# A hybrid decoder layer on one core: split x kept in DRAM between two sweeps, gates written as tanh, another order in the passage to the output projection

## The chip, the cores and the metric

The kernel runs on one core of a Trainium2 chip. The metric is the device time of one execution in microseconds (us). The profile comes from one execution recorded by the hardware profiler.

## What is computed

One step of a decoder layer, on 2048 prompt tokens and 8 × 4 decode tokens with 1024 channels. Cut from the reference:

```python
xn = rms_norm(x, p['g_mix_norm'])
proj = xn @ p['w_in']                      # u_pool 256 | x_rnn 512 | g_rnn 512 | q 256
o_pool, new_pool = pool_mixer(ctx_pool, u_pool, start, p['w_pool'], p['pool_scale'])
xc, new_conv = causal_dwconv(ctx_conv, x_rnn, p['rnn_conv_w'], p['rnn_conv_b'])
h, h_last = rg_lru(xc, h0, p['w_rg_a'], p['b_rg_a'], p['w_rg_x'], p['b_rg_x'], p['rg_lambda'])
o_rnn = jax.nn.gelu(g_rnn, approximate=True) * h
o_xa = cross_attn(q, mk, mv)               # 4 heads, 256 memory tokens
mix = jnp.concatenate([group_rms(o_pool), group_rms(o_rnn), group_rms(o_xa)], axis=-1)
x = x + (mix * p['g_mix_out']) @ p['w_out']
xn = rms_norm(x, p['g_ffn_norm'])
gate_c, new_ffn = causal_dwconv(ctx_ffn, xn @ p['w_ff_gate'], p['ffn_conv_w'], p['ffn_conv_b'])
x = x + (jax.nn.gelu(gate_c, approximate=True) * (xn @ p['w_ff_up'])) @ p['w_ff_down']
# rg_lru:  r = sigmoid(xb @ w_a + b_a);  i = sigmoid(xb @ w_x + b_x)
#          log_a = -8 * r * softplus(-lam);  a = exp(log_a);  mult = sqrt(-expm1(2 * log_a))
#          h_t = a_t * h_(t-1) + mult * i * xc
```

## The kernel before

Channels lie on the 128 partitions and tokens on the free axis. The tokens are cut into 6 stages of 344 or 348 columns (`NCOL`; the 32 decode tokens lie at the start of stage 0), and two stages make a block. Every matrix product is made in fp32r from a rounded part and a rest: ACT writes the part (`hi`, tiles `ah..`, `h_w..`), DVE the rest (`lo`, tiles `al..`, `l_w..`), and PE does three matmuls, hi·hi, lo·hi and hi·lo.

The program runs through these phases; the times are read off the trace of PE:

- *First sweep*, 5 to 252 us, stages 0 to 5. `g_prep` loads x of a stage and splits it, with the gain g_mix, into 8 pairs `ahr`, `alr`. PE makes the recurrent input (`pr`, weights wr0 to wr3) and the gate branch (`pq`, wr4 to wr7). DVE and ACT do the convolution (`xc`), PE the small gate matmuls (`pg`, L452), ACT the sigmoids `r`, `i` (L455), then tanh, exp, square and square root (L466 to L472) and GELU (L556); DVE does the scan.
- *Memory keys and values* (`pkv`), 252 to 263 us.
- *Second sweep*, 263 to 437 us, stages 0 to 5 again: x is loaded and split once more (`ahp`, `alp`, L127 and L128), PE makes q and the pooling input (`pf`, `pq`, `pu`), then attention (`pS`, `pT`, `pV`), the decode attention (`pSd`, `pTd`, `pVd`) and the pooling product.
- *Passage*, 438 to 525 us: the output projection of block 0 (`po`, d = 0 to 7), with y = x + result, the squares `sq` and their sum `ssa`; the four stores of `ys` by SP (L1371); and the first weights of the next part, raw (`wr11o`, `wr12o`, `wr21o`, `wr22o`), formed into sums `s1o` to `s4o` and split into `wt..`.
- *Planned part*, 526 to 2110 us: the output projection of blocks 1 and 2 and the feed-forward part, by seven products (numbers 0 to 6) on half matrices in place of eight, `Block` for activations (`h0s`..`h6s`, `l0s`..`l6s`) and `Pair` for weights. Product i accumulates in a PSUM bank, `"abcbbac"[i]`: products 0 and 5 share bank a, and after product 0 ACT copies bank a to bank b (`post`, printed as `bo<-ao`).

What stands where: PE and SP follow the written program order throughout. In the two sweeps a hand-made weaver (class `Weave`, with the table `W` of waits) sets at which point between the matmuls of the projections a generator makes its next step. ACT, DVE and POOL are ordered by a scheduler up to the passage and are in written order from there on. SP issues its DMAs strictly in that order and stops at the first one whose data or buffer is not ready.

Of the kernel before, what the change touches and what calls it, by code (L numbers as in the profile page):

```python
# [43 lines left out]
def hybrid_kernel(ctx: ExitStack, tc: tile.TileContext, I, O):  # L44
# [140 lines left out]

    xs = I["x"]
# [57 lines left out]
    def g_prep(st, src, n, g, name, parts=2, wait=1.2, pool=0):  # L244

        x = big([P, 8, n], "x" + name)
        st += [x, [pair(f"{name}{k}", n) for k in range(KD // 2)]]
        w = KD // parts
        for k in range(KD):
            if k == 0 or (parts > 2 and k % w == 0):  # L250
                for h in range(k, k + w if parts > 2 else KD, w):
                    nc.sync.dma_start(out=x[:, h:h + w, :], in_=src[:, h:h + w, :])
# [192 lines left out]
    def g_gates(s, c2, n, st):  # L445

        xc, r, ii = st["xc"], st["r"], st["i"]
        dec = s == 0
        for c in (2 * c2, 2 * c2 + 1):
            pg = [psC(f"pg{s}{c}{h}") for h in range(2)]  # L450
            for h in range(2):
                T.matmul(pg[h][:, 0:n], bdg[half(h), c, :], xc[half(h), c, :], start=True, stop=True)  # L452
            for d, (dst, bias) in enumerate(((r, "ba"), (ii, "bx"))):
                for h in range(2):
                    S.activation(out=dst[half(h), c, :], in_=pg[h][half(d ^ h), 0:n], func=AF.Sigmoid,  # L455
                                 bias=pcol(bias, c)[half(h)])
            if c % 2:
                V.tensor_tensor(out=ii[:, c - 1:c + 1, :], in0=ii[:, c - 1:c + 1, :], in1=xc[:, c - 1:c + 1, :],
                                op=ALU.mult)
            yield 0.6, W["g2"]  # L460
        if c2 == 1:
            th = xc
            a2 = big([P, 4, n], f"a2{s}")

            for c in range(4):
                S.activation(out=th[:, c, :], in_=r[:, c, :], func=AF.Tanh, scale=sc8[:, c:c + 1])  # L466
            a = st["a"] = r
            for c in range(4):
                S.activation(out=a[:, c, :], in_=r[:, c, :], func=AF.Exp, scale=nl[:, c:c + 1])
            S.activation(out=a2, in_=a, func=AF.Square)  # L470
            V.scalar_tensor_tensor(out=th, in0=a2, scalar=1.0, in1=th, op0=ALU.add, op1=ALU.mult)
            S.activation(out=th, in_=th, func=AF.Sqrt)  # L472
            V.tensor_tensor(out=ii, in0=ii, in1=th, op=ALU.mult)
            if dec:
                d0 = kp.tile([P, 4, NB], F32, name="d0")
                V.tensor_tensor(out=d0, in0=t0(a), in1=h0, op=ALU.mult)
                V.tensor_tensor(out=t0(ii), in0=t0(ii), in1=d0, op=ALU.add)
                V.memset(t0(a), 0.0)

    for s in range(NS):  # L480
# [7 lines left out]
        if s + 1 < NS:  # L488
            xq[s + 1] = []
            pg_ = g_prep(xq[s + 1], x_src(s + 1), NCOL[s + 1], "g_mix", f"r{s + 1}", 2, W["prep_r"])  # L490
# [4 lines left out]
        else:  # L495
            wq, wkv, xm, xp = [], [], [], []
# [3 lines left out]
            gp = g_prep(xp, x_src(0), NCOL[0], "g_mix", "p0", 2)  # L500
        st = {k: tmp("t", [P, 4, n], f"{k}{s}") for k in ("xc", "r", "i")}
        xc = st["xc"]
        for c2 in range(2):
# [131 lines left out]
    def g_attn(s, n, npr, p0, qd, qs):  # L635
# [25 lines left out]
        def transp(j):  # L661
            e, c0, w = es[j]
            e_done.append(e)
            for mc in range(2):
# [41 lines left out]
    def g_dec(qd, ox):  # L706
# [28 lines left out]
        for mc in range(2):  # L735
            T.transpose(pT[:, mc * P:(mc + 1) * P], e[:, 0, mc * P:(mc + 1) * P], ident)
            pt4 = pT[:, mc * P:(mc + 1) * P].rearrange("p (g b m) -> p g b m", g=4, b=2)
# [22 lines left out]
    for s in range(NS):  # L760
# [28 lines left out]
        split(*qs, q[:, :, p0:n], G if W["n_q"] else V)  # L789
# [59 lines left out]
        wv.add(g_pool(s, n, npr, p0, df), W["pool" if s else "pool_0"])  # L849

# [50 lines left out]
    ys = [[dr.tile([P, 2, 2, NCOL[2 * b]], F32, name=f"ys{b}{j}") for j in range(4)] for b in range(NBLK)]  # L901
# [39 lines left out]
    class Block:  # L941
# [45 lines left out]
    class Pair:  # L987
# [7 lines left out]
        def load(self):  # L995
# [3 lines left out]
            for i, x in ((2, 1), (2, 2), (1, 1), (1, 2)):  # L999
# [103 lines left out]
    def out_stage(b):  # L1103
        n = NCOL[2 * b]
        stages.append(("out", b, len(D), 2, src_mix(b)))
        for d in range(2):
# [8 lines left out]
            def residual(d=d):  # L1115
                for j in (2 * d, 2 * d + 1):
                    for h in range(2):
                        nc.sync.dma_start(out=ys[b][j][:, :, h, :], in_=x_src(2 * b + h)[:, 2 * j:2 * j + 2, :])

            at[N + 3].append(residual)  # L1120
            at[N + 5].append(begin)
# [165 lines left out]
    order = [[0, 2, 1, 5, 3, 6, 4]] * (len(D) - 1) + [[0, 2, 1, 5, 3, 4, 6]]  # L1287
# [18 lines left out]
    for d in range(len(D)):  # L1306
        for s in range(2):
            p = D[d][s]
            N = 14 * (d - 1)
            put(N + (0, 5)[s], p.load)  # L1310
            for i, x in zip((1, 2, 3, 4), (8, 10, 12, 14) if p.make else (4, 6, 9, 12)):
                put(N + x + s, lambda p=p, i=i: p.sigma(i))
                if p.make:
                    put(N + x + s + 2, lambda p=p, i=i: p.keep(i))
            for i in range(7):
                if d == i == 0:
                    continue
                put(pos(d, s, i) - AH - 1, lambda p=p, i=i: p.hi(i))
                put(pos(d, s, i) - AH, lambda p=p, i=i: p.lo(i))
# [40 lines left out]
    def sq0(j):  # L1360

        for d in (2 * j, 2 * j + 1):
            q = wp.tile([P, 2, n], F32, tag="w", bufs=16, name=f"sq0{d}")
            S.activation(out=q, in_=y[d], func=AF.Square)
            if "a0" not in ssum:
                ssum["a0"], first = f1.tile([P, 2, n], F32, tag="ss", bufs=1, name="ssa0"), q
            elif d == 1:
                V.tensor_tensor(out=ssum["a0"], in0=first, in1=q, op=ALU.add)
            else:
                V.tensor_tensor(out=ssum["a0"], in0=ssum["a0"], in1=q, op=ALU.add)  # L1370
        nc.sync.dma_start(out=ys[0][j], in_=yt[j // 2][:, 2 * (j % 2):2 * (j % 2) + 2])  # L1371
# [15 lines left out]
    for d in range(4, KD):
# [19 lines left out]
    sq0(3)  # L1407
# [11 lines left out]
    early.sort(key=lambda z: z[0])  # L1419
    for x0, x1, i in ((-99, -6, 2), (-6, -2, 1), (-2, 0, None)):  # L1420
        for x, f in early:
            if x0 <= x < x1:
                f()
        if i is not None:
            B0.hi(i)
            B0.lo(i)
# [191 lines left out]
```

## Time and profile before

| | |
|---|---|
| median of 3 runs | 2127.59 us (2126.03 to 2129.19) |
| profiled execution | 2129.87 us, span 2128.0 us |
| mean granted TensorE clock | 0.984 |
| PE busy | 2065.4 us, 97% of the span |
| DVE busy, ACT busy | 1633.5 us (77%), 1323.1 us (62%) |
| ACT table loads | 31, of 1283 ns each |
| DMA | 408.72 MB, mean 192 GB/s |

Engines in the rows are PE (matmul), PEld (weight load), DVE, ACT, POOL and SP; an ending q marks the engine's sequencer, where DMA issues stand. A row of the timeline reads: start, duration, engine, line, operation, out<-in, shapes, count, and in brackets the idle time ahead of it with what ended it. A stretch with idle time of PE is a wait; a stretch of low granted clock is one in which PE is busy and each matmul takes longer.

### The profile page before, as it was taken

What the parts mean: (1) busy time and instruction counts of PE and PEld (TensorE: products, weight loads), DVE (VectorE), ACT (ScalarE), POOL (GpSimd) and SP (SyncE); (2) the same over time, 40 slices, a digit from 0 to 9 for tenths busy, and PEclk for the clock granted to TensorE, in tenths of its full rate; (3) what the DMA queues carried; (4) which work ended last, traced back from release to release, by engine and by line L of the source; (5) the groups of instructions that cost most, each with busy time, mean ns of one, the idle gap of its engine ahead of it and who ended that gap; (6) DMA issues with size and microseconds to landing.
All of it is one profiled execution on the core that took longest, in us unless ns stands there. A gap on an engine that the chain in (4) does not pass through costs nothing.

```text
span 2128.0 us, 35270 instructions
## 1 busy us (share of the span) xinstructions
PE 2065.4 (97%) x12996; PEld 2009.0 (94%) x12996; DVE 1633.5 (77%) x2846; ACT 1323.1 (62%) x2380; POOL 69.3 (3%) x82
## 2 busy tenths in 40 slices
PE   8999998998999999999999999999999999999997
PEld 7888887888999999999999999999999999999997
DVE  7886897874878988889888666668778666668774
ACT  7879954552566656566655665557666665557663
POOL 0000000000000000000000000000000000000001
PEclk9999999999999999999999999999999999999998
DMA  4112342235997656677997555677887554677882
GB/s 144 55 55 90 126 169 85 66 111 199 286 305 232 229 194 217 197 242 219 260 262 230 188 187 162 211 261 223 245 248 186 190 191 158 217 261 221 247 226 86
DMA packets 257804, 408.72 MB, mean 192 GB/s; under 512 B 24416, under 2 KB 123456, under 8 KB 257632
## 3 DMA queue, kind: packets, MB, share of 16 engines
q1 hardware_dynamic: 242640, 367.19, 52.7%
q0 software_dynamic: 13760, 37.77, 8.4%
q8 instruction: 102, 1.67, 0.3%
q10 hardware_dynamic: 1232, 1.51, 0.2%
q14 instruction: 70, 0.57, 0.1%
HBM read 289.17 MB, written 122.92 MB: 194 GB/s over the span
## 4 chain that ended last, share of the span: by engine, by line
PE 80%; DVE 7%; ACT 5%; DMA 5%; issue 2%; SPq 0%; POOL 0%; POOLq 0%; DVEq 0%; ACTq 0%
PE bu L1054 9%; PE bg L1054 9%; PE bd L1054 9%; PE ag L1054 6%; PE cg L1054 6%; PE ad L1054 6%; PE cu L1054 6%; PE au L1054 6%; PE cd L1054 6%; PE pq L227 3%; PE po L227 2%; PE pu L227 2%; PE pr L227 1%; PE pf L227 1%; ACT r L455 1%
## 5 line engine op out<-in xcount | busy, mean ns | idle before, releaser
L1158 DVE SCALAR_TENSOR_TENSOR cv<-gt,pv,cv 128x696 f32<-128x696 f32 (+2 forms) x144 | 133.0, 924 | 34.9 <-ACT cv L1153 34.9
L1174 DVE TENSOR_TENSOR u<-u,cv 128x696 f32<-128x696 f32 (+1 forms) x72 | 63.3, 879 | 62.7 <-ACT cv L1170 62.7
L1220 POOL DMA_DIRECT2D ys<-cd x32 | 35.0, 1138 | 1367.2 <-ACT cd L1083 894.1
L1054 PE MATMUL bd<-h4s,wt4d 128*128 128x348 f32 (+1 forms) x288 | 72.8, 326 | 4.2 <-DVE cd L1076 4.2
L1054 PE MATMUL ag<-h5s,wt5g 128*128 128x348 f32 (+1 forms) x288 | 74.8, 322 | 0.0
L1054 PE MATMUL bg<-h4s,wt4g 128*128 128x348 f32 (+1 forms) x288 | 74.6, 322 | 0.0
L1054 PE MATMUL bg<-h1s,wt1g 128*128 128x348 f32 (+1 forms) x288 | 74.5, 322 | 0.0
L1054 PE MATMUL bg<-h3s,wt3g 128*128 128x348 f32 (+1 forms) x288 | 74.5, 322 | 0.0
L1054 PE MATMUL cu<-h6s,wt6u 128*128 128x348 f32 (+1 forms) x288 | 74.5, 321 | 0.0
L1054 PE MATMUL ag<-h0s,wt0g 128*128 128x348 f32 (+1 forms) x288 | 74.5, 321 | 0.0
L1054 PE MATMUL cg<-h6s,wt6g 128*128 128x348 f32 (+1 forms) x288 | 74.5, 321 | 0.0
L1054 PE MATMUL bu<-h4s,wt4u 128*128 128x348 f32 (+1 forms) x288 | 74.4, 321 | 0.1
L1054 PE MATMUL cg<-h2s,wt2g 128*128 128x348 f32 (+1 forms) x288 | 74.4, 321 | 0.0
L1054 PE MATMUL au<-h5s,wt5u 128*128 128x348 f32 (+1 forms) x288 | 74.4, 320 | 0.0
L1054 PE MATMUL au<-h0s,wt0u 128*128 128x348 f32 (+1 forms) x288 | 74.4, 320 | 0.0
L1054 PE MATMUL cu<-h2s,wt2u 128*128 128x348 f32 (+1 forms) x288 | 74.4, 320 | 0.0
L1054 PE MATMUL bu<-h1s,wt1u 128*128 128x348 f32 (+1 forms) x288 | 74.3, 321 | 0.0
L1054 PE MATMUL bu<-h3s,wt3u 128*128 128x348 f32 (+1 forms) x288 | 74.3, 321 | 0.0
L1054 PE MATMUL bd<-h3s,wt3d 128*128 128x348 f32 (+1 forms) x288 | 71.9, 322 | 2.1 <-ACT t6d L1072 2.1
L1054 PE MATMUL cd<-h6s,wt6d 128*128 128x348 f32 (+1 forms) x288 | 73.4, 326 | 0.0
L227 PE MATMUL pr<-ahr,h_wr 128*128 128x348 f32 (+1 forms) x192 | 64.8, 338 | 8.5 <-ACT ahr L127 8.5
L1054 PE MATMUL ad<-h0s,wt0d 128*128 128x348 f32 (+1 forms) x288 | 71.5, 321 | 0.0
(552 smaller groups left out, 7549.3 us busy)
## 6 DMA issues: line engine op xcount, KB each, us to landing
hs<-u SPq DMA_DIRECT2D x24, 696.0 KB, 4.1
ys<-cd POOLq DMA_DIRECT2D x20, 696.0 KB, 11.3
wr22g<-in_w_gate_dram SPq DMA_DIRECT2D x36, 256.0 KB, 4.1
wr11g<-in_w_gate_dram SPq DMA_DIRECT2D x36, 256.0 KB, 4.6
wr12g<-in_w_gate_dram SPq DMA_DIRECT2D x36, 256.0 KB, 4.7
wr22u<-in_w_up_dram SPq DMA_DIRECT2D x36, 256.0 KB, 6.5
wr11u<-in_w_up_dram SPq DMA_DIRECT2D x36, 256.0 KB, 6.6
wr12u<-in_w_up_dram SPq DMA_DIRECT2D x36, 256.0 KB, 6.2
```

What stands on the lines that cost most here:

```text
L227: T.matmul(o, w_[:, ks], z, start=(k == 0 and i == 0), stop=(k == nk - 1 and i == 2))
L455: S.activation(out=dst[half(h), c, :], in_=pg[h][half(d ^ h), 0:n], func=AF.Sigmoid, bias=pcol(bias, c)[half(h)])
L1054: T.matmul(pt[:, 0:n], w[:, w_, ks_(k)], blk.hl[i][a_][:, k, :], start=(i in (0, 2) and k == m == 0), stop=(k == 3 and m == 2), skip_group ...
L1158: V.scalar_tensor_tensor(out=cv[:, z0:nn], in0=gt[:, z0 + t:nn + t], scalar=pcol("fcw", 3 * f + t), in1=cv[:, z0:nn], op0=ALU.mult, op1=AL ...
L1174: V.tensor_tensor(out=u, in0=u, in1=k["cv"][:, i, 0:nn], op=ALU.mult)
L1220: at[N + 14 + 1 + s].append(lambda j=2 * d + s, k=ks[s]: G.dma_start(out=flat(ys[b][j]), in_=qv(k["c"], n), accum_op=ALU.add, max_dma_last ...
```

## The change

1. In the first sweep `g_prep` gets `keep`: after each odd k, SP stores the pair's hi and lo tile in DRAM (`xhl`), 48 stores. The second sweep takes the tiles back with 8 loads per stage (`load_parts`) and splits nothing.
2. The sigmoids become tanh(0.5·z); the missing half and one are put into the other constants (`gb`, `sc8`, the factor of the square root), and DVE multiplies (i + 1)·xc in one instruction. ACT's table loads go from 31 rows to 20 in the order.
3. `gate` in `W` goes from 6.8 to 8.2, `g2` from 0 to 1.4.
4. The two decode transposes `pTd` stand together ahead of the copies out of their bank.
5. The copies of x to `ys` of blocks 1 and 2 (16 DMAs, DRAM to DRAM, formerly in the out stages) are issued by SP in the second sweep, in stages 1 and 2.
6. In the passage the stores of `ys` of block 0 go by POOL's queue, the squares use other buffers, one at a time; the raw first weights lie in another pool; the tiles of the activations are placed by hand; the first out step takes its products in the order 0, 5, 2, 1, 3, 6, 4 and loads (1,2) first.

SP at the start. `st_wr` is a raw weight, `xr` a quarter of x of stage 0. Before:

```order
L135 DMA st_wr_107<-in_w_in_dram 128x512
L252 DMA xr_113<-in_x_dram 128x688
L135 DMA st_wr_107<-in_w_in_dram 128x512
L252 DMA xr_113<-in_x_dram 128x688 x3
L135 DMA st_wr_166<-in_w_in_dram 128x1024
```

Now, with `xhl` the kept tiles in DRAM:

```order
L135 DMA st_wr_125<-in_w_in_dram 128x512
L255 DMA xr_131<-in_x_dram 128x688
L260 DMA xhl_81<-ahr_132 128x688
L260 DMA xhl_81<-alr_133 128x688
L135 DMA st_wr_125<-in_w_in_dram 128x512
L255 DMA xr_131<-in_x_dram 128x688
L260 DMA xhl_81<-ahr_134 128x688
L260 DMA xhl_81<-alr_135 128x688
L255 DMA xr_131<-in_x_dram 128x688
L260 DMA xhl_81<-ahr_136 128x688
L260 DMA xhl_81<-alr_137 128x688
L255 DMA xr_131<-in_x_dram 128x688
```

After two more stores the weights wr1 to wr3 follow. Each load of x but the first now stands behind the stores of the quarter before it.

ACT at the end of stage 0's gates; `ahr_231` is the last pair of x of stage 1, `r` and `xc` are the gates' tiles, `g` the gate branch. Before:

```order
L469 ACT_TABLE_LOAD
L469 ACTIVATE r_238<-r_238,sp 128x344
L466 ACTIVATE xc_237<-r_238,sc_163 128x344 x2
L469 ACTIVATE r_238<-r_238,sp 128x344 x3
L556 ACT_TABLE_LOAD
L556 ACTIVATE g_407<-g_407 128x1376
L470 ACTIVATE a_513<-r_238 128x1376
L127 ACTIVATE ahr_231<-xr_224,pv 128x344
```

Now the last pair (`ahr_259`) stands ahead of the first gate, and no table load stands between the gates, their tanh and exp:

```order
L127 ACTIVATE ahr_259<-xr_252,pv 128x344
L467 ACTIVATE r_266<-pg_506,gb 64x344
L467 ACTIVATE r_266<-pg_507,gb 64x344
L467 ACTIVATE i_267<-pg_506,gb 64x344
L467 ACTIVATE i_267<-pg_507,gb 64x344
```

The split of the next stage's x moved from behind the gates to the front of them.

ACT at the first out step, from behind the last square on; `h2s` is the hi part of activation 2, `wt2o` a split weight. Before:

```order
L975 ACTIVATE h2s_5519<-q12s_5227 128x1392
L1035 ACTIVATE wt2o_5525<-s1o_5523 128x512
L1035 ACTIVATE wt2o_5533<-s1o_5527 128x512
L1035 ACTIVATE wt1o_5535<-s2o_5530 128x512
L975 ACTIVATE h1s_5541<-q11s_5231 128x1392
L1035 ACTIVATE wt1o_5549<-s2o_5538 128x512
L1035 ACTIVATE wt5o_5551<-wr12o_5509 128x512
L975 ACTIVATE h5s_5557<-q21s_5228 128x1392
L1035 ACTIVATE wt5o_5565<-wr12o_5517 128x512
L1064 ACTIVATE bo_5588<-ao_5575 128x348
```

Now:

```order
L985 ACTIVATE h5s_5521<-q21s_5236 128x1392
L1045 ACTIVATE wt5o_5541<-wr12o_5523 128x512
L1045 ACTIVATE wt5o_5544<-wr12o_5531 128x512
L985 ACTIVATE h2s_5517<-q12s_5235 128x1392
L1045 ACTIVATE wt2o_5551<-s1o_5547 128x512
L1045 ACTIVATE wt2o_5556<-s1o_5554 128x512
L1045 ACTIVATE wt1o_5564<-s2o_5561 128x512
L985 ACTIVATE h1s_5515<-q11s_5239 128x1392
L1045 ACTIVATE wt1o_5579<-s2o_5566 128x512
L1074 ACTIVATE bo_5602<-ao_5589 128x348
```

What product 5 needs moved to the front; the copy of bank a still stands in tenth place.

The diff, cut to its core:

```diff
-             norm_0=9.35, stat_0=2.55, prep_m=2.07, kv=11.0, gate=6.8, norm=14.0, stat=8.5, prep_r=9.7, mix_r=10.2,
+             norm_0=9.35, stat_0=2.55, prep_m=2.07, kv=11.0, gate=8.2, norm=14.0, stat=8.5, prep_r=9.7, mix_r=10.2,
...
+    xhl = [dr.tile([P, 2, 8, n], F32, name=f"xhl{s}") for s, n in enumerate(NCOL)]
...
+            split_g(hi, lo, x[:, k, :], pcol(g, k))
+            if k % 2 and keep is not None:
+                for i in range(2):
+                    nc.sync.dma_start(out=keep[:, i, k - 1:k + 1], in_=st[1][k // 2][i].bitcast(F32))
             yield 0.0, wait
+
+    def load_parts(s):
+
+        x = [pair(f"p{s}{k}", NCOL[s]) for k in range(KD // 2)]
+        for k in range(KD // 2):
+            for i in range(2):
+                nc.sync.dma_start(out=x[k][i].bitcast(F32), in_=xhl[s][:, i, 2 * k:2 * k + 2])
+        return [None, x]
...
-                    S.activation(out=dst[half(h), c, :], in_=pg[h][half(d ^ h), 0:n], func=AF.Sigmoid,
-                                 bias=pcol(bias, c)[half(h)])
+                    S.activation(out=dst[half(h), c, :], in_=pg[h][half(d ^ h), 0:n], func=AF.Tanh, scale=0.5,
+                                 bias=gb[half(h), bias + c:bias + c + 1])
...
         for mc in range(2):
             T.transpose(pT[:, mc * P:(mc + 1) * P], e[:, 0, mc * P:(mc + 1) * P], ident)
+        for mc in range(2):
             pt4 = pT[:, mc * P:(mc + 1) * P].rearrange("p (g b m) -> p g b m", g=4, b=2)
...
-            pg_ = g_prep(xq[s + 1], x_src(s + 1), NCOL[s + 1], "g_mix", f"p{s + 1}", 2, W["prep_p"], W["n_prep"])
...
+            xq[s + 1] = load_parts(s + 1)
...
+        if 0 < s < NBLK:
+            for j in range(4):
+                for h in range(2):
+                    nc.sync.dma_start(out=ys[s][j][:, :, h, :], in_=x_src(2 * s + h)[:, 2 * j:2 * j + 2, :])
...
-    order = [[0, 2, 1, 5, 3, 6, 4]] * (len(D) - 1) + [[0, 2, 1, 5, 3, 4, 6]]
+    order = [[0, 5, 2, 1, 3, 6, 4]] + [[0, 2, 1, 5, 3, 6, 4]] * (len(D) - 2) + [[0, 2, 1, 5, 3, 4, 6]]
...
-        nc.sync.dma_start(out=ys[0][j], in_=yt[j // 2][:, 2 * (j % 2):2 * (j % 2) + 2])
+        if d % 2:
+            G.dma_start(out=ys[0][d // 2], in_=yt[d // 4][:, d % 4 - 1:d % 4 + 1])
```

More of the change, by code (lines that the diff above doesn't have):

```diff
@@ L242, in psC, with g_prep @@
         return ps.tile([P, 512], F32, tag="C", bufs=4, name=name)
[L244 removed]
+    def g_prep(st, src, n, g, name, parts=2, wait=1.2, keep=None):
         x = big([P, 8, n], "x" + name)
@@ L1113, in begin @@
                     k["c"] = quad(f"co{b}{d}{s}")
[L1115 to L1121, printed above, removed]
+            at[N + (5 if N else 2)].append(begin)
             for s in range(2):
@@ L1297, in hybrid_kernel, with put @@
     NWT, NRAW, AH = 8, 12, 6
-    early = []
-    def put(x, f):
+    early = {}
+    def put(x, f, what, s):
         if x < 0:
-            early.append((x, f))
+            early[what, s] = f
         else:
@@ L1358, in hybrid_kernel, with sq0 @@
     n = NCOL[0]
[L1360 to L1371, printed above, removed]
+    def sq0(d):
+        q = wp.tile([P, 2, n], F32, tag="stg", bufs=3, name=f"sq0{d}")
+        S.activation(out=q, in_=y[d], func=AF.Square)
+        if d == 0:
+            ssum["a0"] = f1.tile([P, 2, n], F32, tag="ss", bufs=1, name="ssa0")
+            ssum["first"] = q
+        else:
+            V.tensor_tensor(out=ssum["a0"], in0=ssum.pop("first") if d == 1 else ssum["a0"], in1=q, op=ALU.add)
+        if d % 2:
+            G.dma_start(out=ys[0][d // 2], in_=yt[d // 4][:, d % 4 - 1:d % 4 + 1])
     ctx.enter_context(tc.manual_schedule(engines={mybir.EngineType.Activation, mybir.EngineType.DVE,
@@ L1418, in hybrid_kernel, with do @@
             T.matmul(t[:, c:c + P], ident, ident, start=(c == 0), stop=(c == 256))
[L1419 to L1426, printed above, removed]
+    for i in (4, 6, 3, 1, 2):
+        B0.place(i)
+    for z in "hl":
+        f2.tile([P, 4, n], F32R, tag=f"{z}0", bufs=1, name=f"{z}0s")
+    B0.place(5)
+    def do(what, s):
+        early.pop((what, s))()
+    for s in range(2):
+        do("load", s)
+    B0.hi(5)
+    B0.lo(5)
+    for s in range(2):
+        do("hi5", s)
+        do("lo5", s)
+    do("sigma1", 0)
+    B0.hi(2)
+    B0.lo(2)
+    for s in range(2):
+        if s:
+            do("sigma1", s)
+        do("hi2", s)
+        do("lo2", s)
+    for i in (1, 2, 3):
+        for s in range(2):
+            if i > 1:
+                do(f"sigma{i}", s)
+            if i < 3:
+                do(f"keep{i}", s)
+            if i == 2 and s == 0:
+                do("hi1", 0)
+    assert not early, early.keys()
     for s in range(2):
         D[0][s].w[0] = D[0][s].w0
-    for x, i in ((0, 5), (2, 3), (4, 6), (6, 4)):
+    for x, i in ((0, 1), (2, 3), (4, 6), (6, 4)):
         at[x].insert(0, lambda i=i: (B0.hi(i), B0.lo(i)))
```

96 lines of the change are left out of this document (43 added, 53 removed).

## The prediction

> **What bounds the kernel now.** I read the share of busy time first, then the two halves of the span, then the idle time of PE row by row. The first fence has the busy line of the page, the split of the span (columns: length, PE busy and instructions, granted clock, DMA share, GB/s), and below that stretches with all engines (PE, PEld, DVE, ACT, POOL busy; then clock, DMA share, GB/s).
>
> ```profile
> PE 2065.4 (97%) x12996; PEld 2009.0 (94%) x12996; DVE 1633.5 (77%) x2846; ACT 1323.1 (62%) x2380; POOL 69.3 (3%) x82
> 0.00:640.00 640.00, 597.36 (x3728) 0.96 0.43 142
> 640.00:2128.00 1488.00, 1468.03 (x9270) 0.99 0.70 214
> 56.00:62.00 6.00, 5.13 (x18) 5.13 (x19) 4.92 (x10) 3.44 (x4) 0.00 (x0) 0.52 0.68 238
> 188.00:196.00 8.00, 8.00 (x30) 6.22 (x29) 7.67 (x23) 7.35 (x13) 0.71 (x1) 0.57 0.25 89
> 239.00:247.00 8.00, 7.71 (x27) 6.78 (x28) 5.96 (x21) 7.80 (x13) 0.56 (x1) 0.57 0.01 1
> 267.00:273.00 6.00, 5.15 (x17) 4.71 (x18) 6.00 (x12) 5.17 (x10) 1.60 (x3) 0.50 1.01 390
> ```
>
> TensorE is the bound everywhere. The change ends before 640 us (its last piece is the residual copies), and up to there PE stands idle for 640.00 − 597.36 = 42.6 us; nothing behind 640 is touched, so I take no time from there. A wait costs more than its own length: after it the granted clock drops to about half for a few us, as the last four rows show, and PE loses about (1 − clock) of each such stretch. The number of matmuls is the same after the change, so only idle time and low-clock time can move.
>
> **The start: a loss.** Each odd k now stores two tiles on SP, in program order between the loads of x. The next fence has SP, then ACT, DVE and PE at the start, the medians to landing, and one SP row from later.
>
> ```profile
> 1.19 0.42 SPq L252 DMA_DIRECT2D xr<-in_x_dram  x1
> 2.12 1.39 SPq L252 DMA_DIRECT2D xr<-in_x_dram  x3
> 3.56 4.07 SPq L135 DMA_DIRECT2D st_wr<-in_w_in_dram  x3
> 4.79 1.05 ACT L127 ACTIVATE ahr<-xr,pv 128x344 fp32r<-128x344 f32 x2 [0.24 <-DMA xr<-in_x_dram]
> 5.53 1.06 DVE L128 SCALAR_TENSOR_TENSOR alr<-xr,pv,ahr 128x344 fp32r<-128x344 f32 x2
> 10.88 1.04 ACT L122 ACTIVATE h_wr<-st_wr 128x1024 fp32r<-128x1024 f32 x1
> 11.95 1.23 DVE L123 TENSOR_TENSOR l_wr<-st_wr,h_wr 128x1024 fp32r<-128x1024 f32 x1
> 13.23 0.43 PE L227 MATMUL pr<-ahr,l_wr 128*128 128x344 f32 x1 [0.33 <-DVE l_wr L123]
> st_wr<-in_w_in_dram SPq DMA_DIRECT2D x7, 512.0 KB, 4.5
> xr<-in_x_dram SPq DMA_DIRECT2D x4, 344.0 KB, 4.8
> 496.82 28.64 SPq L1371 DMA_DIRECT2D ys<-y  x4
> ```
>
> Before, all four x chunks are issued by 3.51 and the weights wr1 to wr3 by 7.63; they fly together. The last row shows what SP does at a store whose data is not there: it sat 28.64 us, and all loads behind it with it. Now the store of alr of chunk 0 waits for DVE at 5.53 + 1.06 = 6.59, and chunk 1 is issued two issue slots later, at 6.59 + 0.42 + 0.43 = 7.45. From the issue of a chunk to its last split it took 6.59 − 1.19 = 5.4; with a slot of 0.43 the period is 5.83, so chunk 2 is issued at 13.3, chunk 3 at 19.1, and wr1 (behind the stores of chunk 3) at 24.9. It lands 4.5 later at 29.4; ACT needs 1.04, DVE 1.23: 31.7. PE did the matmul that needs l_wr at 13.23, right behind that DVE row. Shift: 31.7 − 13.23 = 18.5. The eight k of the first 128 outputs lie inside this time and hide nothing of it, since PE has nothing else in its order. Behind the gap a low-clock spell comes as at 56:62, 6.00 × (1 − 0.52) = 2.9; small waits at 13 to 27 (1.4 in sum) go, as ACT and DVE have caught up. **+20**. If each chunk takes the median 4.8 instead of the 3.6 of the first, three chunks add 3.6; if the splits come 1 us sooner in a quiet DVE, 3 go: 17 to 24. The later stages' stores wait on SP too, but nothing urgent is queued behind them.
>
> **The boundary of stages 0 and 1, and the gates.** ACT, then PE, then the group of all gate matmuls:
>
> ```profile
> 54.60 0.57 ACT L127 ACTIVATE ahr<-xr,pv 128x344 fp32r<-128x344 f32 x1
> 55.22 0.66 PE L227 MATMUL pr<-ahr,h_wr 128*128 128x344 f32 x1 [3.04 <-ACT ahr L127]
> 56.87 0.65 PE L227 MATMUL pr<-alr,h_wr 128*128 128x344 f32 x1 [1.00 <-DVE alr L128]
> 185.77 0.85 PE L452 MATMUL pg<-xc,bdg 64*128 64x348 f32 x4 [1.01 <-DVE xc L532]
> L452 PE MATMUL pg<-xc,bdg 64*128 64x348 f32 (+1 forms) x96 | 26.0, 531 | 5.2 <-DVE xc L532 3.2 <-ACT i L455 1.0 <-ACT xm L344 0.5
> ```
>
> The last split of x1 stood behind all gates of stage 0 on ACT; in the new order it stands ahead of them. 3.04 + 1.00 + 2.9 of clock = **−7**. What is late next there is the gates themselves, which no early matmul needs.
>
> The group of pg waits 5.2 in all, mostly on the convolution's xc on DVE. With gate 6.8 to 8.2 and g2 0 to 1.4, 6 to 12 other matmuls (about 0.16 each at full clock, 1 to 2 us) come ahead, so waits of 0.5 to 1 are covered. The two spells at 188 and 239, quoted first, cost 8.00 × 0.43 = 3.4 each, one at 150 half of that. If all goes: 5.2 + 8.5 = 13.7. If the new order only moves the waits: 0. I take a little over half, **−8**, since xc's DVE chain (7.67 of 8.00 busy at 188) is not shortened itself. Eleven table loads fewer, 1.28 each, free 14 us of ACT, which is not the bound; they count only by these waits. Against them the gates' pointer scale adds 0.1 us to some ACT instructions off the path: 0.
>
> One rule speaks against the clock part. The Trainium skill, "TensorE: Matmul & The Clock Gate" (Part 1: The HAM clock gate), puts the drop to half after an idle window of about 3.4 us; here the clock read 0.57 from 188 on with 1.01 as the longest wait shortly before. By that rule the spells at 150, 188 and 239 are not due to these waits and would stay, and this term would be −3; by the rows it is −8, which I keep.
>
> **The second sweep.** Rows of PE and ACT, and the stretch behind the wait at 348:
>
> ```profile
> 263.41 0.40 PE L227 MATMUL pf<-ahp,h_wq 128*128 128x344 f32 x1
> 267.00 0.65 PE L227 MATMUL pf<-alp,h_wq 128*128 128x344 f32 x1 [2.38 <-DVE alp L128]
> 269.08 0.66 PE L227 MATMUL pf<-alp,h_wq 128*128 128x344 f32 x1 [0.85 <-DVE alp L128]
> L127 ACT ACTIVATE ahp<-xp,pv 128x348 fp32r<-128x348 f32 (+1 forms) x44 | 22.8, 583 | 4.4 <-DMA xp<-in_x_dram 2.9 <-PE pu L227 1.5
> 348.57 0.47 PE L736 MATMUL pTd<-ident,ed 128*128 128x128 f32 x1 [5.15 <-DVE wz L739]
> 348.00:352.00 4.00, 3.43 (x15) 3.22 (x15) 1.84 (x7) 1.09 (x2) 0.00 (x0) 0.57 0.00 0
> 492.12 0.81 PE L298 MATMUL bcx<-ident,rsx 116*128 116x116 f32 x3 [4.59 <-DVE rsx L151]
> ```
>
> Splits of x (some 23 us of ACT, as much of DVE) go; the eight parts of a stage come by SP. The first stage waited for its splits, 2.38 + 0.85, with 6.00 × 0.50 = 3.0 of clock: 6.2 at most. The tiles for its parts come free as the first sweep's last matmuls end, some 12 us ahead of the first pf at 263.41; eight loads of 344 KB at 390 GB/s (the 267 row) take 7.2 us, and one takes 4.8 to land. Just in time: **−5**. For later stages the parts are asked for a stage (an estimate of 27 us, the sweep's length over six) ahead; in stages 1 and 2 the eight copies of x stand on SP ahead of the next parts and take half of that lead at most, by the SP rows of the last part below. The second decode transpose no longer stands behind the four copies of the first: 5.15 and 4.00 × 0.43 = 1.7 of clock, **−7**. Short waits on ACT and DVE in this sweep, 0.3 to 0.9 each and 3.2 in all: **−2**, an estimate. The wait at 492 comes from DVE standing in an order that stays (a weight split ahead of rsx): 0.
>
> **The passage and the first out stage.** Rows of ACT, DVE, SP and PE:
>
> ```profile
> 525.52 0.42 SPq L1008 DMA_DIRECT2D wr21o<-in_w_out_dram  x1
> 525.84 1.35 ACT L975 ACTIVATE h2s<-q12s 128x1392 fp32r<-128x1392 f32 x1
> 527.22 1.61 DVE L979 TENSOR_TENSOR l2s<-q12s,h2s 128x1392 fp32r<-128x1392 f32 x1 [0.34 <-ACT h2s L975]
> 530.51 0.69 DVE L1024 TENSOR_TENSOR s1o<-wr21o,wr22o 128x512 f32<-128x512 f32 x1 [1.68 <-DMA wr22o<-in_w_out_dram]
> 531.30 0.63 ACT L1035 ACTIVATE wt2o<-s1o 128x512 fp32r<-128x512 f32 x1 [4.11 <-DVE s1o L1024]
> 531.98 0.43 PE L1054 MATMUL co<-h2s,wt2o 128*128 128x348 f32 x1 [2.07 <-ACT wt2o L1035]
> 536.16 0.95 PE L1054 MATMUL co<-h2s,wt2o 128*128 128x348 f32 x2 [3.60 <-DVE wt2o L1039]
> 540.14 0.44 ACT L1064 ACTIVATE bo<-ao 128x348 f32<-128x348 f32 x1
> 568.57 4.53 SPq L1118 DMA_DIRECT2D ys<-in_x_dram  x4
> 590.73 0.53 PE L1054 MATMUL bo<-h4s,wt4o 128*128 128x348 f32 x1 [4.02 <-DVE co L1076]
> ```
>
> Now the stores of y are on POOL's queue, and SP reaches the weights wr some 9 us sooner. PE waited 2.07 + 3.60 for what was made of them, and a spell of 8 us at 0.57 as the quoted ones, 3.4: 9.1 if it all goes. But product 5 is second now, and it adds into the bank of product 0, which ACT must first have copied out (the bo<-ao row). In ACT's new order that copy stands behind h5, two wt5, h2, two wt2, wt1, h1, wt1. Worked through with the rows: the square of the last y ends at 525.9, h5 at 527.2, l5 on DVE 1.61 later at 528.8, two lo of 0.60 to 530.1, s1o 530.7, l2 532.3, a lo and the second s1o 533.5, one more lo, two s2o 535.4; ACT's wt1 of the first, h1 (1.35), wt1 of the second end at 537.3, the copy at 537.8. PE is through with product 0 at 529.9 (its row before is 2.07 of idle ahead of 531.98): 7.9 idle instead of 5.7, the same spell of clock behind. **+2.4**; −9 if the copy's place does no harm, +6 if the sums s1o wait for POOL's last store.
>
> The residual copies, four issues of 1.1 us of SP at each of four places from 544 to 623 with 13.8 to landing, leave this stretch. The wait of 4.02 at 590 hangs on a weight load that SP issued late behind them, and 1.7 of clock follows: **−5.7**. The same sixteen issues are 18 us of SP in stages 1 and 2 of the second sweep, 9 in each, of 27.
>
> **The sum:** +20 − 7 − 8 − 5 − 7 − 2 + 2.4 − 5.7 = −12.3. The profiled execution took 2129.9 us (span 2128.0 and 1.9 around it): 2117.6. It lies 2.3 above the median of the runs, so I predict 2115.3.
>
> **Rivals.** *Parts come late (slower).* In the second sweep loads of parts share SP and DMA with the copies of x, with kc, vc and upd, and the 267 row shows the DMA share at 1.01 already. If each of five stage starts waits for its part, one landing of 4.8 and a spell of 2.9, it costs 38 and the time is 2153; from 2.5 us per stage on, the kernel is slower. For it: full DMA at 267. Against it: a lead of a stage, and 2.8 MB of parts with 2.8 MB copied, read and written, are 8.4 MB in 27 us or 311 GB/s, where 390 was reached. Chance 0.15.
> *The stores at the start do not hold SP as long* (splits come sooner, weights land within a chunk's round trip): three chunks at 3.6 instead of 5.83 give +11, the time 2106. The SP row at 496.82 is against it. 0.10.
> *The passage gains*: the copy of product 0 is no wait, −9 in place of +2.4: 2104. It needs ACT some 8 us ahead of where its rows put it. 0.12.
> *All spells go with their waits in the gates* (−13.7 and not −8): 2109.6, within the forecast's own range. *The low clock at the gates stays*, because something other than these waits brings it: −3 in place of −8, 2120.3. 0.10. The rule of the Trainium skill named above would give this case.
> *No change in sum*: the start costs 24, the gates give 0, the time is 2127. 0.08.
>
> **How the numbers follow.** The forecast, 2115.3 with a range of its own of 2108 to 2122 (start 17 to 24, gates 0 to −13.7), has 0.45. What a measurement tells from no change is 0.2%, 4.3 us. Faster: 0.45 + 0.10 + 0.12 + 0.10 = 0.77, less a little for forecasts that fall in part, 0.74; same 0.10; slower 0.16. The range goes from 2100 to 2133, which leaves out the worst of the late parts and a case in which start and passage gain at once.
>
> **What would show it.** The first chunk of x issued at 1.2 and the fourth not before 17; PE idle for some 14 to 20 us before 32; no gap behind the last matmul of stage 0; clock at 1.0 where pg waits were; no pf wait at the start of the second sweep; pTd without idle; a wait of 6 to 9 us of PE on ACT's copy ahead of product 5; no wait for co at the second out step. A start gap under 10, or idle of over 2 us at stage starts of the second sweep, would make the prediction wrong.

## The result, and the profile after

The changed kernel is slower: 2144.71 us against 2126.81 us, ratio 1.0078 with a 95% interval of 1.0061 to 1.0094. I had forecast 2115.3 with a range of 2100 to 2133. The profiled execution has a span of 2142.7 us instead of 2128.0, so 14.7 us are to be found.

The span of the changed kernel, split at the first matmul of `ag`, with which the out stages end (length, PE busy and instructions, granted clock, DMA share, GB/s):

```profile
0.00:664.22 664.22, 604.44 (x3781) 0.97 0.53 177
664.22:2142.70 1478.48, 1459.18 (x9217) 0.99 0.70 214
```

Up to `ag` PE is now idle for 59.8 us. In the kernel before, where `ag` starts at 648.36, it was 42.6. Behind it no new wait appears: PE is idle for 19.3 us there, and was for 20.0. To place the loss I take the first matmul of each phase on PE and compare its start with that of the kernel before:

| first matmul of | before | after | shift | this piece | forecast |
|---|---|---|---|---|---|
| `pr` of stage 1 | 48.70 | 68.54 | +19.8 | start +19.8 | +20 |
| `pkv` | 251.57 | 276.11 | +24.5 | rest of the first sweep +4.7 | −15 |
| `pq` of the second sweep, stage 2 | 340.47 | 363.05 | +22.6 | start of the second sweep −2.0 | −5, −2 |
| `pu` of stage 2 | 365.09 | 380.78 | +15.7 | decode transposes −6.9 | −7 |
| `po` | 437.77 | 453.32 | +15.6 | rest of the second sweep −0.1 | 0 |
| `bprime` (behind the last `po`) | 524.04 | 542.17 | +18.1 | passage +2.6 | 0 |
| second out step | 561.68 | 583.31 | +21.6 | first out step +3.5 | +2.4 |
| `ag` (end of the out stages) | 648.36 | 664.22 | +15.9 | wait at 590 gone −5.8 | −5.7 |

Up to the last instruction 1.2 us more come back. Five pieces are as forecast within 1.2 us. The sum was −12.3 and the span grew by 14.7, an error of 27.0. Most of it, 19.7 us, is one piece, the first sweep behind its start; 5.0 more are the start of the second sweep and 2.6 the passage.

The start, on SP and on PE of the changed kernel:

```profile
1.19 0.42 SPq L255 DMA_DIRECT2D xr<-in_x_dram  x1
7.62 0.47 SPq L255 DMA_DIRECT2D xr<-in_x_dram  x1
13.25 0.46 SPq L255 DMA_DIRECT2D xr<-in_x_dram  x1
18.94 0.45 SPq L255 DMA_DIRECT2D xr<-in_x_dram  x1
24.65 1.52 SPq L135 DMA_DIRECT2D st_wr<-in_w_in_dram  x3
11.81 0.65 PE L230 MATMUL pr<-ahr,h_wr 128*128 128x344 f32 x1 [3.71 <-ACT ahr L127]
30.19 0.66 PE L230 MATMUL pr<-ahr,h_wr 128*128 128x344 f32 x1 [4.56 <-ACT h_wr L122]
31.45 0.66 PE L230 MATMUL pr<-ahr,l_wr 128*128 128x344 f32 x1 [0.32 <-DVE l_wr L123]
```

The four chunks of x are issued 6.43, 5.63 and 5.69 us apart, a round trip each, and the weights at 24.65. The matmul that stood at 13.23 stands at 31.45: 18.2 later, where the sum had 18.5. Behind the gap a matmul of PE takes 0.49 us up to 36.5 and 0.32 from there on, so the slow spell of some 6 us came as forecast, although the granted clock of the rows reads 1.00 from 30 to 36.

The rest of the first sweep: DVE, then PE, then the stretch behind the first of these waits (length, PE busy and instructions, clock, DMA share, GB/s). `sqr` are the squares of the next stage's x, `str` is their sum over the channels, made by PE.

```profile
83.58 0.83 DVE L570 TENSOR_TENSOR_SCAN xc<-r,hcar,i 128x312 f32<-128x312 f32 x1
84.45 1.58 DVE L355 TENSOR_TENSOR sqr<-sqr 128x1392 f32<-128x1392 f32 x1
88.91 0.51 DVE L345 TENSOR_TENSOR sqr<-sqr 128x348 f32<-128x348 f32 x1
89.56 0.71 PE L160 MATMUL str<-ones,sqr 128*116 128x1 f32 x3 [5.40 <-DVE sqr L345]
168.24 0.74 PE L160 MATMUL str<-ones,sqr 128*116 128x1 f32 x6 [2.76 <-DVE sqr L345]
171.49 1.53 PE L464 MATMUL pg<-xc,bdg 64*128 64x348 f32 x4 [1.93 <-DVE xc L545]
252.20 1.53 PE L464 MATMUL pg<-xc,bdg 64*128 64x348 f32 x4 [2.91 <-DVE xc L545]
266.00 0.94 PE L464 MATMUL pg<-xc,bdg 64*128 64x348 f32 x4 [2.13 <-DVE xc L545]
89.00:93.00 4.00, 3.44 (x14) 0.50 0.09 32
```

The wait for `ahr` early in stage 1 is gone, as forecast. In its place PE waits 5.40 for the squares of stage 2's x. They stand on DVE behind the scan of stage 0, and the scan stands at the end of the gate chain: gate matmul, ACT's gates, tanh, exp, square, root, then DVE. Before, no `str` waited at all. The clock fell to 0.50 behind the waits at 89.56, 171.49 and 252.20, but not behind the 2.13 at 266.00, where it reads 1.00 from 265 to 270.

The second sweep and the passage of the changed kernel, PE, ACT and DVE:

```profile
312.33 0.46 ACT L309 ACTIVATE rbp<-bcp 128x348 f32<-128x348 f32 x1 [4.23 <-DVE upd L833]
312.84 0.40 PE L661 MATMUL pS<-kTh,qs 64*104 64x256 f32 x1 [2.06 <-ACT rbp L309]
365.73 0.38 PE L742 MATMUL pTd<-ident,ed 128*128 128x128 f32 x2
507.90 1.23 DVE L123 TENSOR_TENSOR l_wo<-st_wo,h_wo 128x1024 fp32r<-128x1024 f32 x1 [2.54 <-ACT h_wo L122]
509.34 0.81 PE L308 MATMUL bcx<-ident,rsx 116*128 116x116 f32 x3 [6.22 <-DVE rsx L151]
555.35 0.61 ACT L1045 ACTIVATE wt1o<-s2o 128x512 fp32r<-128x512 f32 x1
555.87 0.44 ACT L1074 ACTIVATE bo<-ao 128x348 f32<-128x348 f32 x1
556.37 0.66 PE L1064 MATMUL ao<-h5s,wt5o 128*128 128x348 f32 x1 [8.33 <-ACT bo L1074]
```

No `pf` waits for its data any more, both transposes go through together, and no product of the second out step waits. New are the wait of 2.06 at `pS`, 1.6 us more at `bcx`, and the wait of PE for the copy of bank a, 8.33 where the sum had 7.9.

### The profile page after: what moved, and what is told of

Its sections match the earlier page's. It is cut to its first block, busy times and chain, and to the rows that moved or that the text cites. A ratio compares the mean times of both kernels' runs of the same rounds, so it can differ in the third digit from the quotient of the medians.

```text
span 2142.7 us, 35290 instructions
## 1 busy us (share of the span) xinstructions
PE 2063.6 (96%) x12996; PEld 2008.2 (94%) x12996; DVE 1614.6 (75%) x2799; ACT 1292.4 (60%) x2321; POOL 71.2 (3%) x86
## 4 chain that ended last, share of the span: by engine, by line
PE 76%; issue 8%; DVE 7%; DMA 4%; ACT 4%; POOL 0%; SPq 0%; POOLq 0%; DVEq 0%; ACTq 0%
PE bg L1064 10%; PE bu L1064 10%; PE bd L1064 7%; PE ag L1064 6%; PE cg L1064 6%; PE cu L1064 6%; PE au L1064 6%; PE ad L1064 5%; PE cd L1064 5%; PE pq L230 3%; PE bo L1064 2%; DMA wr11d<-in_w_down_dram 1%; PE co L1064 1%; PE ao L1064 1%; PE pu L230 1%
## 5 line engine op out<-in xcount | busy, mean ns | idle before, releaser
L1178 DVE TENSOR_TENSOR u<-u,cv 128x696 f32<-128x696 f32 (+1 forms) x72 | 63.3, 879 | 63.2 <-ACT cv L1174 63.2
L1064 PE MATMUL bd<-h1s,wt1d 128*128 128x348 f32 (+1 forms) x288 | 71.5, 321 | 0.0
```

The lines of the kernel that those rows point to most:

```text
L1064: T.matmul(pt[:, 0:n], w[:, w_, ks_(k)], blk.hl[i][a_][:, k, :], start=(i in (0, 2) and k == m == 0), stop=(k == 3 and m == 2), skip_group ...
L1178: V.tensor_tensor(out=u, in0=u, in1=k["cv"][:, i, 0:nn], op=ALU.mult)
```

## The experiments

Theory A: the later gate matmuls lengthen the gate chain, and the next stage's DVE work behind the scan comes late. Theory B: the tanh form gives ACT and DVE a worse order. Theory C: the stores hold SP back all through the sweep. Times of the kernel before in these comparisons were 2129.4 to 2130.2 us, so the ratio counts.

### gates_old: the old spacing in the changed kernel

```diff
-gate=8.2 ... g2=1.4
+gate=6.8 ... g2=0
```

> The changed kernel with the gates' old spacing (gate 6.8, g2 0) and all else as changed. Theory A (spacing): placing the gate matmuls 6 to 12 matmuls later delays ACT's gate chain and with it DVE's scan; the next stage's squares and convolution stand behind the scan on DVE, and PE waits for them (str 5.40 at 89.56, 2.76 at 168.24, pg 2.91 at 252.20, 2.13 at 266.00). Then the first pkv comes at 260 to 268 instead of 276.1, and the time is 2130 to 2136. Theory B (tanh): the waits come from the order that the scheduler gives ACT and DVE with the tanh form; nothing moves, 2143 to 2146. Theory C (stores): the stores of the split tiles hold SP and the next stage's x all through the sweep; nothing moves either, 2143 to 2146.

Measured: 2137.61 us, ratio 1.0032 (1.0016 to 1.0048), span 2135.3; `pkv` starts at 267.36. 7.4 us of span come back; at `pkv` it is 8.8. PE's waits in that sweep:

```profile
88.56 0.74 PE L160 MATMUL str<-ones,sqr 128*116 128x1 f32 x6 [3.63 <-DVE sqr L345]
91.49 1.52 PE L464 MATMUL pg<-xc,bdg 64*128 64x344 f32 x4 [1.44 <-DVE xc L545]
167.63 1.16 PE L464 MATMUL pg<-xc,bdg 64*128 64x348 f32 x4 [2.11 <-DVE xc L545]
254.93 0.94 PE L464 MATMUL pg<-xc,bdg 64*128 64x348 f32 x4 [0.95 <-DVE xc L545]
```

The time is a little above the 2130 to 2136 of theory A. The waits late in the sweep shrink; the one at 89 falls from 5.40 to 3.63, but 1.44 comes behind it, and stage 1 takes 43.8 us where it took 44.0. So A holds for the later stages; the wait in stage 1 has another cause. The scan of stage 4 in the changed kernel and in this run:

```profile
241.03 3.43 DVE L570 TENSOR_TENSOR_SCAN xc<-r,hcar,i 128x348 f32<-128x348 f32 x4
231.90 3.44 DVE L570 TENSOR_TENSOR_SCAN xc<-r,hcar,i 128x348 f32<-128x348 f32 x4
```

The first matmul of stage 5 stands at 230.79 and at 228.30, so the scan starts 10.2 us into the stage with the new spacing and 3.6 us with the old one.

### spacing_alone: the new spacing in the kernel before

```diff
-gate=6.8 ... g2=0
+gate=8.2 ... g2=1.4
```

> The kernel before with only the new spacing (gate 8.2, g2 1.4). Theory A: the waits for pg shrink, but the gate chain ends later and str and xc waits take their place, first pkv at 258 to 264 instead of 251.6, the time 2133 to 2139. Theories B and C: the spacing is not what costs, pg waits shrink, 2121 to 2128.

Measured: 2145.20 us, ratio 1.0062 (1.0041 to 1.0083), `pkv` at 259.17, 7.6 later than before. With sigmoids, without stores, the same waits appear:

```profile
69.69 1.29 PE L160 MATMUL str<-ones,sqr 128*116 128x1 f32 x6 [5.64 <-DVE sqr L335]
235.12 1.53 PE L452 MATMUL pg<-xc,bdg 64*128 64x348 f32 x4 [2.92 <-DVE xc L532]
276.69 0.66 PE L227 MATMUL pf<-alp,h_wq 128*128 128x344 f32 x1 [3.08 <-DVE alp L128]
```

5.64 and 2.92 are near the 5.40 and 2.91 of the changed kernel. B and C cannot make them here. The first is not a later chain: the last square ends at 69.54, and at 69.37 in the kernel before. With the new spacing alone, too, the last split of stage 1's x stands ahead of the gates on ACT, PE no longer waits for it and comes to `str` sooner. The second is a later chain. One edit of two numbers, which I had put at −8, costs the kernel before 0.6%, more than theory A had.

### tanh_alone: the gates as tanh in the kernel before

```diff
-S.activation(out=dst[...], in_=pg[h][...], func=AF.Sigmoid, bias=pcol(bias, c)[half(h)])
+S.activation(out=dst[...], in_=pg[h][...], func=AF.Tanh, scale=0.5, bias=gb[half(h), bias + c:bias + c + 1])
```

(and the constants and DVE's multiply, as in the change)

> The kernel before with only the gates as tanh (fewer table loads on ACT, sigmoid gone, the factors in the other constants). Theory A: the gate chain gets shorter by up to two table loads a stage, first pkv at 240 to 248 instead of 251.6, the time 2114 to 2123. Theory B: the new order on ACT and DVE makes the waits for sqr and xc, 2130 to 2140. Theory C: no stores, little moves, 2122 to 2127.

Measured: 2120.62 us, ratio 0.9963 (0.9946 to 0.9980), `pkv` at 246.99. The tanh form gains, against theory B. But it does not gain all that it frees:

```profile
67.34 1.32 PE L160 MATMUL str<-ones,sqr 128*116 128x1 f32 x6 [4.02 <-DVE sqr L335]
262.71 0.42 PE L227 MATMUL pf<-alp,h_wq 128*128 128x344 f32 x1 [0.89 <-DVE alp L128]
```

Here the gates end early and the spacing is the old one, and still PE, which no longer stops early in stage 1, stops 4.02 us at the next `str`. That is as much as the 3.04 and 1.00 that went, given back with the old spacing too. Stage 1 takes 45.0 us where it took 43.3. And the wait for `alp` at the start of the second sweep falls from 2.38 and 0.85 to 0.89 without any kept part.

### late_stores: the stores of stage 0 behind the first loads

```diff
-                for i in range(2):
-                    nc.sync.dma_start(out=keep[:, i, k - 1:k + 1], in_=st[1][k // 2][i].bitcast(F32))
+                store() if late is None else late.append(store)
...
     nc.sync.dma_start(out=xrd, ...)
+    for store in late:
+        store()
```

> The changed kernel with the eight stores of stage 0 issued by SP behind the loads of x, wr1 to wr3, bdg, h and xrd, and not between them. If the start costs what the first rows say (the first matmul with l_wr of the second weight at 31.45 instead of 13.23), that matmul is back at 13 to 14, everything behind it is 18 to 20 us earlier, and the time is 2124 to 2127. Rival: the chain of ACT and DVE sets the first sweep, and PE's late start was its cover; then half comes back, about 2135, with longer waits for sqr and xc. Theory C (stores hold SP in all stages) says a gain of under 20 as well, since stages 1 to 5 keep theirs.

Measured: 2129.85 us, ratio 1.0003 (0.9989 to 1.0016), span 2127.3, 15.4 less. The matmul with the second `l_wr` is back at 13.52. The time is above the 2124 to 2127 expected: some of the gain is lost at once, because the eight stores now stand on SP ahead of wr4 to wr7 and of stage 1's x:

```profile
31.41 0.66 PE L230 MATMUL pq<-ahr,l_wr 128*128 128x344 f32 x1 [3.87 <-DVE l_wr L123]
60.54 0.66 PE L230 MATMUL pr<-ahr,h_wr 128*128 128x344 f32 x1 [4.79 <-ACT ahr L127]
153.34 0.84 PE L160 MATMUL str<-ones,sqr 128*116 128x1 f32 x6 [2.76 <-DVE sqr L348]
250.44 0.96 PE L470 MATMUL pg<-xc,bdg 64*128 64x348 f32 x4 [2.14 <-DVE xc L551]
```

The waits at 153 and 250 are those of the changed kernel at 168 and 266, to a hundredth. From the first `pr` of stage 1 to `pkv` it is 207.3 us, and 207.6 in the changed kernel: the late start covered nothing.

### copy_early: ACT's copies of bank a ahead in the first out step

```diff
+    def rest():
+        do("sigma1", 0)
+        ...
+    at[2] = [rest] + at[0] + at[1] + at[2]
+    at[0], at[1] = [], []
```

> The changed kernel, with ACT's copies of product 0 ahead of h2, wt2, wt1 and h1 in the first out step (all that product 5 does not need is written behind product 0). Theory: PE's 8.33 us ahead of product 5 is the place of the copy in ACT's order; it falls to 0 to 3, and the time is 2136 to 2140. Rival: the sums s1o and the lo parts on DVE are late in any case, the wait only moves to product 2, and the time stays at 2142 to 2146.

Measured: 2139.42 us, ratio 1.0049 (1.0032 to 1.0065), span 5.7 less than the changed kernel. Product 5 starts without a wait; the largest one left in this step is for product 1:

```profile
547.10 0.44 ACT L1074 ACTIVATE bo<-ao 128x348 f32<-128x348 f32 x1
559.01 0.42 PE L1064 MATMUL bo<-l1s,wt1o 128*128 128x348 f32 x1 [1.22 <-DVE l1s L989]
```

So the 8.33 was the place of the copy in the written order. The edit also moves sums and rests of DVE back, but what the wait ended with was ACT's copy, which now stands at 547.10. The new product order no longer costs PE this wait once the copy is moved.

### three_fixes: old spacing, early copy, stores behind all first loads

The edits above, with the stores of stage 0 issued after stage 1's x.

> The changed kernel with three edits: old spacing of the gates, ACT's copies early, and the stores of stage 0 behind all first loads (wr4 to wr7 and x of stage 1 too, as with the stores ahead of these PE waited 3.87 for wr5 and 4.79 for x of stage 1). If the parts are what they were singly, the span is 2142.7 - 7.4 (spacing) - 20 (start) - 6 (copy) = 2109, the time 2108 to 2114, clear of the kernel before. Rival: the late start was the cover of ACT and DVE in the first sweep; then waits for sqr and xc grow and the time is 2118 to 2126.

Measured: 2109.19 us, ratio 0.9901 (0.9877 to 0.9924), span 2106.5: a little under the 2109 that the parts add up to. It is faster than both kernels. The waits of over 1 us that it keeps in the first 300 us, behind the first load:

```profile
69.12 0.77 PE L160 MATMUL str<-ones,sqr 128*116 128x1 f32 x6 [1.12 <-DVE sqr L348]
72.05 1.47 PE L468 MATMUL pg<-xc,bdg 64*128 64x344 f32 x4 [1.57 <-DVE xc L551]
147.59 0.86 PE L468 MATMUL pg<-xc,bdg 64*128 64x348 f32 x4 [2.13 <-DVE xc L551]
282.51 0.36 PE L667 MATMUL pS<-kTh,qs 64*104 64x256 f32 x1 [2.06 <-ACT rbp L312]
```

### three_fixes_g54: the gate matmuls closer still

```diff
-gate=6.8
+gate=5.4
```

> three_fixes with the gate matmuls closer still (gate 5.4 instead of 6.8). Theory A, if earlier is better all the way: the scan ends sooner, the waits of pg and str for DVE shrink, 2 to 6 us below three_fixes. Rival: at 6.8 the two sides are balanced, and PE now waits at pg for xc or ACT instead: 2 to 8 us above three_fixes.

Measured: 2111.33 us, ratio 0.9906 (0.9878 to 0.9935): not told apart from three_fixes. PE now waits 5.81 at the `pg` of stage 1, for xc, and 0.8 to 1.0 at most others:

```profile
70.54 1.52 PE L468 MATMUL pg<-xc,bdg 64*128 64x344 f32 x4 [5.81 <-DVE xc L551]
```

The wait has changed its place from `str` to `pg`. It is longer than the 1.12 and 1.57 of three_fixes; three_fixes_bcast, with the same instructions in this sweep as three_fixes, has 4.03 at `str`, so the size varies between runs. Both ends read DVE work behind the same scan.

### three_fixes_bcast: a later broadcast in the second sweep

```diff
-bc_p=1.0
+bc_p=6.0
```

> three_fixes with the broadcast of the second sweep's next stage five units later (bc_p 6.0 instead of 1.0). PE waited 2.05 to 2.06 us at pS for ACT's copy rbp, which waits for a DVE instruction behind the pooling sums, and the clock fell for some us. Theory: the wait comes from the bank that the early broadcast holds; it goes, 3 to 5 us below three_fixes. Rival: pS waits for something else at the same place, within 1 us of three_fixes.

Measured: 2104.45 us, ratio 0.9881 (0.9846 to 0.9915); the interval covers that of three_fixes, so whether it is faster than that is unclear. The theory fell in part: the wait at `pS` is gone, but a longer one stands at the broadcast itself. From `pkv` to `po` this run takes 181.0 us, and three_fixes 175.8: the second sweep got longer. What the profile gains is in the passage (77.3 us from `po` to `bprime` in place of 87.7), where the wait at `bcx` (4.80 in three_fixes) is gone. That the edit does this is not shown, so if the run is faster by the 3 to 5 us expected, it is not by the mechanism expected. The row of the broadcast:

```profile
290.65 0.84 PE L311 MATMUL bcp<-ident,rsx 116*128 116x116 f32 x3 [5.51 <-ACT e L643]
```

### resplit: three_fixes without the kept parts

No stores of split tiles; the second sweep loads x and splits it again, by the lines of the kernel before.

> three_fixes without the kept parts: no stores of split tiles, and in the second sweep x is loaded and split again as before the change. Theory: the kept parts pay at the start of the second sweep (waits of 3.2 for alp, and the low clock behind) and a little by less work on ACT and DVE; without them pf starts where it did in three_fixes and loses 4 to 7 us by the second q, the time is 2113 to 2119. Rival: the parts cost as much as they save (SP, DMA, the wait of 2.06 at pS), and the time is 2106 to 2111, as three_fixes.

Measured: 2109.54 us, ratio 0.9909 (0.9884 to 0.9933). The rival was right: keeping the parts is worth nothing that can be measured. In the traces the parts take 1.5 us off the way from the first `pf` to the first `pq` (16.9 in three_fixes, 18.4 here), and add 4.2 from there to the first `pu` (15.3 and 11.0), where three_fixes has its wait at `pS` and this run has none. The wait that they take away is this one:

```profile
264.45 0.43 PE L230 MATMUL pf<-alp,h_wq 128*128 128x344 f32 x1 [0.88 <-DVE alp L128]
```

### transposes_alone

```diff
         for mc in range(2):
             T.transpose(pT[:, mc * P:(mc + 1) * P], e[:, 0, mc * P:(mc + 1) * P], ident)
+        for mc in range(2):
             pt4 = ...
```

> The kernel before with only the two decode transposes ahead of the copies. Theory: the wait of 5.15 at 348.57 and the low clock behind it go, nothing takes their place, 2118 to 2122. Rival: the copies of DVE are needed next by pVd and PE waits there instead, 2124 to 2128.

Measured: 2122.01 us, ratio 0.9961 (0.9945 to 0.9977). Between the `pq` and the `pu` around the place the shift goes from +3.3 to −3.5, 6.9 us, and no wait takes its place. The +3.3 arose in the first sweep, where the two kernels have the same instructions (see the last section).

## Why the prediction was wrong

The working named the start as the largest term and had its size: +20, and +19.8 by the first matmul of stage 1. The decode transposes (−7, measured −6.9), the copies of x (−5.7, −5.8) and the first out step (+2.4, +3.5) are right by place and size. Two of them were tested alone, the transposes in the kernel before and the copy of bank a late in ACT's order by moving it; no run moves the copies of x alone.

The step that failed is "**The boundary of stages 0 and 1, and the gates**", −7 and −8. It went wrong in two ways.

- For the −7, I asked what is late next and answered "the gates themselves, which no early matmul needs". The next in line was `str`, which needs the squares, which stand on DVE behind the scan, at the end of the gate chain. Taking PE's wait away brings PE to `str` sooner, while the chain moves little. tanh_alone shows it without the stores and the spacing. The scan of stage 0, the last square and `str`, the first three rows of the kernel before and the last two of tanh_alone (its `str` is shown above):

```profile
59.61 0.86 DVE L559 TENSOR_TENSOR_SCAN xc<-r,hcar,i 128x312 f32<-128x312 f32 x1
68.86 0.51 DVE L335 TENSOR_TENSOR sqr<-sqr 128x348 f32<-128x348 f32 x1
71.17 0.67 PE L160 MATMUL str<-ones,sqr 128*116 128x1 f32 x6
58.51 0.86 DVE L563 TENSOR_TENSOR_SCAN xc<-r,hcar,i 128x312 f32<-128x312 f32 x1
66.78 0.51 DVE L335 TENSOR_TENSOR sqr<-sqr 128x348 f32<-128x348 f32 x1
```

PE reaches `str` at 67.34 − 4.02 = 63.3 and no longer at 71.2, 7.9 us sooner; the squares end only 2.1 us sooner. In the changed kernel stage 1 takes 44.0 us where it took 43.3: +0.7 in place of −7.
- For the −8, I took the spacing as cover for PE alone and let it cost nothing. A later gate matmul is also a later start of a chain that ends in the scan, by 6.6 us in stage 5, as gates_old shows. I had seen that DVE was busy for 7.67 of 8.00 us near 188 and drew from it only that the gain might be halved. spacing_alone turns the sign: `pkv` is 7.6 us later by the spacing alone, and gates_old gives 7.4 us of span back. "If the new order only moves the waits: 0" was no bound from below, since a loss was not excluded. From the first matmul of stage 2 to `pkv` it is 159.6 us before and 163.6 in the changed kernel, +4.0 in place of −8. In gates_old and in tanh_alone it is 154.3: the tanh form gains 5.3 us there, and the spacing costs 9.3 on top of it.

The second sweep's start had −5 for waits of `pf`, and −2 for short ones; 2.0 of the 7 were seen. The waits for `pf` went, and from the first `pf` to the first `pq` it is 16.9 us in place of 23.0. But from there to the first `pu` it is 16.8 in place of 11.1, since the wait of 2.06 at `pS` came, with the clock at 0.50 behind it:

```profile
314.00:318.00 4.00, 4.00 (x15) 0.50 1.07 315
```

And the credit went to the wrong part of the change: most of the wait for `pf` goes with the tanh form (0.89 left in tanh_alone, 0.88 in resplit). The passage had 0 for the `bcx` wait, since its order stays. It grew from 4.59 to 6.22, because a weight split ahead of it on DVE waits for ACT's hi part, which waited for its load. SP issued that load 15.2 us later than before, and PE was 15.6 later there, so it was not issued late; why it took longer was not tried. In tanh_alone, with the passage as before, the wait is 5.47, so a part of the growth may not come from the change.

The rivals: the kernel is slower, but not by "parts come late"; the parts were there in time. Its 2153 lies nearest to the measured time by luck. "No change in sum", with the gates at 0, was nearest in mechanism; it had 0.08, and its 2127 is 18 us short. That the gates' term could be a loss was in no rival.

Two small sums of the prediction do not come out of their terms. 7.9 − 5.7 is +2.2 and not +2.4 for the first out step. In the second rival, three chunks that are 2.23 shorter take 6.7 from the 20 of the start, which leaves +13 and not +11. Neither changes what follows.

The clock rule. By the rows a wait of 1 to 2 us can drop the clock. By the Trainium skill, "TensorE: Matmul & The Clock Gate" (Part 1: The HAM clock gate), it takes an idle window of about 3.4 us, in a window that runs freely. The runs agree with neither as a fixed price. In transposes_alone a wait of 1.98, shorter than that window, brought 0.50 (the wait and the stretch behind it: length, PE busy, clock, DMA share, GB/s):

```profile
40.78 2.08 PE L452 MATMUL pg<-xc,bdg 64*128 64x344 f32 x4 [1.98 <-ACT i L455]
42.00:44.00 2.00, 2.00 (x7) 0.50 0.00 0
```

In three_fixes the wait of 2.13 at 147.59, shown above, brought nothing:

```profile
150.00:154.00 4.00, 4.00 (x27) 1.00 0.21 78
```

A price of 3 us for the clock behind every short wait, as I used it, is too sure.

## What to carry to other kernels

When a wait of the bounding engine is taken away, follow the other engines' order to the next thing that it needs and ask where that stands now; a wait removed ahead of a slow chain reappears at the chain's end. A number that delays an instruction has two prices, that of the engine which no longer waits for it and that of everything behind it, so its sign is open until the chain is followed to its last reader. And on an engine that issues in order, put stores behind the loads that the first work needs: stores put between the first loads cost 18 us here, and moving them, with the old spacing and the earlier copy, turned a loss of 0.8% into a gain of 1.0%.

## What was not expected of the hardware

A spell of low clock can come and go with one load. In stage 0 of transposes_alone ACT waited 2.08 us for x of stage 1, and 0.63 in the kernel before with the same instructions there, and its first gate stands at 39.08 where it stood at 36.48. So the `pg` at 40.78 waited 1.98, and the clock was at 0.50 from 42 to 48; in the kernel before, waits of 0.81 and 0.19 left it at 1.00. With 1.4 us from first loads that landed later, this puts the run 4.75 us behind at the first matmul of stage 1. Stage 1 gives 1.4 back, and +3.3 us go into the second sweep, half of the effect under test.
